# Two transformer blocks with a mixture of experts on one core: expert weights loaded in rows twice as long

## The chip, the core and the metric

The kernel runs on one core of a Trainium2 chip. Its engines work beside each other and wait for each other by semaphores: TensorE (PE in the profile; PEld is its loading of weights), VectorE (DVE), ScalarE (ACT), GpSimd (POOL) and SyncE (SP), which here issues nearly all transfers. Sixteen DMA engines move the data between HBM and SBUF. The metric is the device time of one execution in microseconds (us), the median over runs.

## The reference

Two transformer blocks over 512 tokens of width 1024, in float32. The first has sparse attention and a linear recurrence, the second an mLSTM, differential attention and then a mixture of 32 experts, of which each token takes two. What the change touches is the weights of these experts:

```
def hierarchical_moe(h, w_rg, b_rg, w_re, b_re, w_gate, w_up, w_down):
    hf = h.reshape(-1, d_)
    ...
    for e in range(N_EXPERTS):                       # 32
        act = jax.nn.silu(hf @ w_gate[e]) * (hf @ w_up[e])       # 1024 -> 256, twice
        y = y + combine[:, e:e + 1] * (act @ w_down[e])          # 256 -> 1024
```

The three matrices of one expert are 3.1 MB, those of all 32 are 100.7 MB. Every one is read once.

## The kernel before

The kernel isn't written in the order in which it runs. `Net` records each operation into a `Plan` (`record`, L230), with its price and the tiles that it reads and writes; `Plan.order` (L264) then lays the operations out on five engines by a model of their times, gives each tile a buffer, and `issue` writes the program. There are two such plans here: blocks and the first round of experts in one, and a loop over further rounds that isn't entered with these inputs.

Buffers come from pools by tag (`SIZES`, L525): t4 has 38 buffers of 4 KB per partition, a2 has 15 and p2 has 9 of 2 KB. A tag keeps a list of its free buffers with the time from which each is free, and an operation that gives birth to a tile takes the first. A load may be placed long before its use, as soon as a buffer is free, but leaves twelve free for work that is nearer (`RES`, `NEAR`), from which the expert weights are let off until some 9000 operations ahead (`FREE`, `FAR`, L413). So expert weights are fetched while the second block still runs. A buffer that is taken again holds its load back until the last reader of its former tile is done: SyncE waits for that reader, most often a matmul, and as SyncE issues in order, all loads behind it wait too. Each load also waits until the load eight places before it has landed.

The blocks work on slabs of weights of 0.524 MB: a load on SyncE into a t4 buffer, a rounded copy (hi, F32R) and the remainder (lo, F32R) by ScalarE, VectorE or GpSimd, then three passes on TensorE (`slab`, L588, and `mm3`). Slabs of the second block's input are gt and gr, of its output gr from in_wo; ada_w is summed by VectorE and ScalarE. Mb is a row of the mLSTM's decays, read from DRAM to all partitions (Md).

The experts come last (`experts`, L1796). An iteration does two experts, i and i + 16, each for 64 token rows, beside each other in the halves of TensorE's array:

- GpSimd gathers 128 token rows into X (two buffers in turn), TensorE transposes them, ScalarE and VectorE scale them into XT.
- Up and gate: for each quarter q of the 1024 rows and each expert one load of 128 partitions x 4 KB (wg, 0.524 MB), and four matmuls into H for a quarter. Eight loads per iteration.
- act = silu(gate) x up, two transposes, a copy to aT.
- Down: for each of two k and two halves h of the columns and each expert one load of 128 partitions x 2 KB (wd, 0.262 MB, half of each 4 KB row in DRAM), and two matmuls. Eight loads per iteration, some into p2 and some into a2.
- VectorE scales the result into Y, and GpSimd adds it to the output rows with a scatter (out_rows).

The lines in the profile are nearly all L409, where a recorded call is made; so the names of the tiles tell the operations apart.

Of the kernel before, what the change touches and what calls it, by code (L numbers as in the profile page):

```python
# [134 lines left out]
class Tile:  # L135
    def __init__(self, plan, tag, shape, dt, name, keep, given=None):
        self.plan, self.tag, self.name, self.dt, self.shape, self.keep = plan, tag, name, dt, list(shape), keep
        self.got = given
        self.space = plan.tags[tag].space
        n = 1  # L140
# [29 lines left out]

class Node:
# [7 lines left out]
class Plan:  # L179
# [20 lines left out]
    def tile(self, tag, shape, dt, name, keep=False):  # L200
        return Tile(self, tag, shape, dt, name, keep).view()
# [62 lines left out]
    def order(self):  # L264
# [9 lines left out]
        for nd in nodes:  # L274
            for t in nd.tiles:
                if id(t) in seen or t.tag not in prof:
                    continue
                seen.add(id(t))
                end = N if t.keep else t.last + 1
                start = 0 if t.placed else t.first  # L280
                prof[t.tag][start:end] += 1
# [3 lines left out]
        for nd in nodes:  # L285
            for t in nd.births:
                rest[t.tag] += not nd.load
# [13 lines left out]
        while len(out) < N:  # L301
# [3 lines left out]
            for e, lst in ready.items():  # L305
# [4 lines left out]
                for nd in lst:  # L310
# [7 lines left out]
                    if nd.births:  # L318
                        ok = nd.load or nd.i - p < 400
                        need = {}  # L320
                        for t in nd.births:
# [11 lines left out]
                            s = max(s, tg.free[k - 1][0])  # L333
# [17 lines left out]
            for t in nd.births:  # L351
# [6 lines left out]
                t.slot = tg.free.pop(0)[1]  # L358
                rest[t.tag] -= not nd.load
                if p < t.first:  # L360
                    prof[t.tag][p:t.first] += 1
# [16 lines left out]
            for t in nd.tiles:  # L378
                t.left -= 1
                if t.left == 0 and not t.keep and self.tags[t.tag].space != "dram":  # L380
                    r = max(k.done[1] + (200.0 if k.done[2] == "PE" or t.space == "psum" else 130.0)
                            for k in [nd] + [k for _, k in t.writes + t.reads])
                    insort(self.tags[t.tag].free, (r, t.slot))
                    if p <= t.last:
                        prof[t.tag][p:t.last + 1] -= 1
# [122 lines left out]
class Net:  # L508
    def __init__(self, tc, ctx, I, out, upto="all", dbg=None):
# [5 lines left out]
        self.kept, self.stand = [], {}  # L515
# [9 lines left out]
    SIZES = {"t4": 38, "a2": 15, "p2": 9, "vm": 4, "sq128": 3, "c1k": 4}  # L525

    def start(self):

        self.nc = Plan(self.tc, self.scratch, self.stand)
        self.nc.tag("dram", "dram", [], self.make)  # L530
# [7 lines left out]
    def make(self, t):  # L538
        if t.space == "dram":
            return self.pools["dram"].tile(t.shape, t.dt, name=t.name)  # L540
        return self.pools[t.space].tile(t.shape, t.dt, name=t.name, tag=f"{t.tag}.{t.slot}", bufs=1)

    def tile(self, tag, shape, dt, name, keep=False, bufs=None, space="sbuf"):
        if tag not in self.nc.tags:
            self.bufs.setdefault(tag, bufs or self.SIZES[tag])
            kept = {t.slot for t in self.kept if t.tag == tag}
            self.nc.tag(tag, space, [k for k in range(self.bufs[tag]) if k not in kept], self.make)
        v = self.nc.tile(tag, shape, dt, name, keep)
# [1247 lines left out]
    def experts(self, first=False):  # L1796
# [8 lines left out]
        for i in range(16):  # L1805
# [29 lines left out]
            for k in range(2):  # L1835
                for h in range(2):
                    for e in range(2):
# [169 lines left out]
```

## Time and profile before

| | us |
|---|---|
| median of 3 runs | 1128.71 (1126.05 to 1131.16) |
| profiled execution, own time | 1124.24 |
| its span | 1122.5 |
| TensorE busy | 1042.7 (93%) |
| VectorE busy | 637.7 (57%) |
| ScalarE busy | 393.3 (35%) |
| GpSimd busy | 187.4 (17%) |

The span runs from the first to the last instruction of the program; 1.7 us lie around it. Busy shares are means over stages that are bound by different things, so the slices and the stretches tell more than the table. In the slices each digit is a tenth of a slice of 28 us, 9 for 90% or more. DMA share is the busy time of the 16 DMA engines over the stretch; it can read a little above 1, since records of packets overlap. A matmul of float32 operands has two records, one of F32R operands has one.

### The profile page before, as it was taken

The page shows a single profiled execution, that of the slowest core. Times are in us where ns is not written, and L with a number is a line of the kernel's source. Part 1 is how long each engine was busy: PE and PEld are TensorE (multiplying, and loading weights), DVE is VectorE, ACT ScalarE, POOL GpSimd, SP SyncE. Part 2 cuts the span into 40 slices and gives each one's busy share as a digit, 9 for nine tenths or more (in the row PEclk, how much of TensorE's full clock was granted, in tenths as well). Part 3 has the DMA queues.
Part 4 walks back from the last instruction along what each step waited for, and adds up shares of the span by engine and source line. Part 5 has one row for each costly group of instructions (what it writes and reads, how often), then busy time and mean ns, then how long its engine had stood idle before and what let it go on. Part 6 is the DMA issues. An engine that isn't in the chain of part 4 may idle for free. (4 is left out here: it accounts for less than half of the span.)

```text
span 1122.5 us, 14439 instructions
## 1 busy us (share of the span) xinstructions
PE 1042.7 (93%) x5172; PEld 722.4 (64%) x5172; DVE 637.7 (57%) x1432; ACT 393.3 (35%) x803; POOL 187.4 (17%) x173
## 2 busy tenths in 40 slices
PE   7999999999999999999999999999996999877875
PEld 5776666777887787786677877788785333322221
DVE  4667789786654746977868877444714223222221
ACT  5326566463222326435653433222422112111110
POOL 1201134001110224401211001100301122210101
PEclk9999989999999999999999999999996999999998
DMA  9981100224345717160232433446699899999995
GB/s 339 344 321 49 39 1 20 75 80 150 113 129 180 259 42 279 63 262 11 94 146 85 160 98 107 171 119 233 235 355 356 323 365 351 350 382 345 387 362 181
DMA packets 77375, 223.43 MB, mean 199 GB/s; under 512 B 12165, under 2 KB 13773, under 8 KB 77297
## 3 DMA queue, kind: packets, MB, share of 16 engines
q1 hardware_dynamic: 72688, 214.04, 53.1%
q0 software_dynamic: 4608, 8.40, 3.0%
q8 instruction: 43, 0.70, 0.3%
q14 instruction: 36, 0.29, 0.1%
HBM read 212.91 MB, written 17.32 MB: 205 GB/s over the span
## 5 line engine op out<-in xcount | busy, mean ns | idle before, releaser
L409 PE MATMUL H<-wg,XT 128*64 128x512 f32 x512 | 128.6, 606 | 10.7 <-DMA wg<-in_wgu 7.7
L409 PE MATMUL b<-hTh,gth 128*128 128x512 f32 x464 | 123.0, 402 | 0.0
L409 PE MATMUL b<-hTl,gth 128*128 128x512 f32 x464 | 121.4, 398 | 0.0
L409 PE MATMUL b<-hTh,gtl 128*128 128x512 f32 x464 | 119.4, 396 | 0.0
L409 PEld LDWEIGHTS b<-hTh,gth 128*128 128x128 f32 x464 | 86.4, 189 | 23.7 <-issue 4.2
L409 POOL TENSOR_TENSOR gtl<-gt,gth 128x1024 fp32r<-128x1024 f32 x23 | 57.4, 2498 | 264.5 <-ACT gth L409 243.8
L409 PEld LDWEIGHTS b<-hTh,gtl 128*128 128x128 f32 x464 | 86.6, 188 | 20.5 <-issue 0.5
L409 PEld LDWEIGHTS b<-hTl,gth 128*128 128x128 f32 x464 | 86.2, 188 | 20.0 <-issue 0.9
L409 PEld LDWEIGHTS H<-wg,XT 128*64 128x64 f32 x512 | 38.1, 138 | 86.3 <-issue 51.9
L409 DVE SCALAR_TENSOR_TENSOR ada_acc<-ada_w,cols,ada_acc 128x1024 f32<-128x1024 f32 x42 | 64.7, 1540 | 7.2 <-DMA ada_w<-in_w_ada 7.1
L409 PE MATMUL b<-wd,aT 128*64 128x512 f32 x256 | 61.7, 613 | 7.3 <-ACT aT L409 4.3
L409 DVE TENSOR_SCALAR XT<-b,mod,mod 128x128 f32<-128x128 f32 x64 | 24.2, 407 | 76.7 <-PE H L409 67.2
L409 PE MATMUL b<-grh,hTh 128*128 128x512 f32 x192 | 57.4, 411 | 6.5 <-ACT grh L409 6.5
L409 DVE SCALAR_TENSOR_TENSOR Y<-b,wt,gate 128x512 f32<-128x512 f32 x32 | 23.9, 751 | 69.3 <-PE b L409 63.1
L409 ACT ACTIVATE XT<-b,mod,mod 128x128 f32<-128x128 f32 x64 | 27.3, 456 | 88.8 <-PE H L409 71.6
L409 ACT ACTIVATE gth<-gt 128x1024 fp32r<-128x1024 f32 x53 | 55.3, 1049 | 7.8 <-DMA gt<-in_wb 7.8
L409 PE MATMUL b<-grl,hTh 128*128 128x512 f32 x192 | 56.5, 405 | 0.0
L409 PE MATMUL b<-grh,hTl 128*128 128x512 f32 x192 | 55.5, 402 | 0.0
L409 POOL DMA_INDIRECT out_rows<-Y,si x16 | 25.3, 1583 | 158.6 <-DVE Y L409 145.8
L409 ACT ACTIVATE grh<-gr 128x1024 fp32r<-128x1024 f32 (+1 forms) x39 | 39.9, 1036 | 31.0 <-DVE gr L409 9.4
L409 DVE TENSOR_TENSOR gtl<-gt,gth 128x1024 fp32r<-128x1024 f32 x35 | 42.6, 1223 | 11.1 <-ACT gth L409 10.4
L409 DVE SCALAR_TENSOR_TENSOR mg<-mg,b 128x512 f32<-128x512 f32 x32 | 21.9, 685 | 43.6 <-PE b L409 43.4
(372 smaller groups left out, 1818.3 us busy)
## 6 DMA issues: line engine op xcount, KB each, us to landing
wg<-in_wgu SPq DMA_DIRECT2D x128, 512.0 KB
wd<-in_wd SPq DMA_DIRECT2D x128, 256.0 KB
gt<-in_wb SPq DMA_DIRECT2D x58, 512.0 KB
ada_w<-in_w_ada SPq DMA_DIRECT2D x48, 512.0 KB
gr<-in_wa SPq DMA_DIRECT2D x23, 512.0 KB
wp<-in_wp SPq DMA_DIRECT2D x16, 512.0 KB
gr<-in_wo SPq DMA_DIRECT2D x16, 512.0 KB
cw<-in_cmp_w SPq DMA_DIRECT2D x8, 512.0 KB
```

Source lines behind the costliest of these rows:

```text
L409: i = getattr(getattr(self.nc, eng), meth)(*[val(a) for a in args], **{k: val(v) for k, v in kw.items()})
```

## The change

Up and gate weights are laid out so that one load brings half of the 1024 rows instead of a quarter: 128 partitions x 8 KB, 1.049 MB, four loads per iteration instead of eight. A down load brings whole rows of 4 KB instead of halves: 0.524 MB, four instead of eight. The bytes are the same.

An 8 KB row needs two 4 KB buffers that lie side by side. So the buffers of t4, a2 and p2 become halves of pairs (2k and 2k + 1), for all tiles of these pools and not for the expert weights alone. A tile of width 2 takes a whole pair that is free; a tile of width 1 takes a half, preferably of a pair that is already in use, and a pair holds tiles of one kind at a time, F32R or other. For this a2 goes from 15 to 16 buffers and p2 from 9 to 8. X0 and X1 become one pair, XT and Y another. Everything else is recorded as before, but the plan is made anew with these rules, so that the order of the whole program and the places of its tiles are others.

```diff
+    def fits(self, k, kind):
+        return k >> 1 not in self.live or self.live[k >> 1][0] == kind
...
+    def pick(self, width, taken, kind):
+
+
+        if width == 1:
+            best = None
+            for r, k in self.free:
+                if k not in taken and self.fits(k, kind) and k ^ 1 not in taken:
+                    half = k >> 1 in self.live
+                    if best is None or r == 0.0 and half > best[2]:
+                        best = r, [k], half
+                    if r > 0.0 or half:
+                        break
+            return best and best[:2]
+        seen = set()
+        for r, k in self.free:
+            if k in taken:
+                continue
+            if k ^ 1 in seen:
+                return r, [k & ~1, k | 1]
+            seen.add(k)
+        return None
...
-                            k = need[t.tag] = need.get(t.tag, 0) + 1
+                            k = need[t.tag] = need.get(t.tag, 0) + t.width
+                            got = tg.pick(t.width, {x for g, x in taken if g == t.tag}, t.kind)
...
-                                    or len(tg.free) < k
+                                    or got is None
...
-                            s = max(s, tg.free[k - 1][0])
+                            s = max(s, got[0])
+                            taken.update((t.tag, x) for x in got[1])
...
-    SIZES = {"t4": 38, "a2": 15, "p2": 9, "vm": 4, "sq128": 3, "c1k": 4}
+    UNITS = {"t4": 1024, "a2": 512, "p2": 512}
+    SIZES = {"t4": 38, "a2": 16, "p2": 8, "vm": 4, "sq128": 3, "c1k": 4}
...
+        u = self.UNITS[t.tag]
+        pair, half = divmod(t.slot, 2)
+        if t.gen not in self.pairs:
+            self.pairs[t.gen] = self.pools[t.space].tile([128, 2 * u], F32, name=t.name, tag=f"{t.tag}.{pair}", bufs=1)
+        a = self.pairs[t.gen][:t.shape[0], half * u:half * u + t.row]
...
-            for q in range(4):
+            for q in range(2):
                 ws = []
                 for e in range(2):
-                    ws.append(self.t4("wg", (128, 2, 512)))
+                    ws.append(self.tile("t4", [128, 4, 512], F32, "wg", width=2))
                     nc.sync.dma_start(ws[e], I["wgu"][i + 16 * e, q])
-                for k in range(2):
-                    kt = 2 * q + k
+                for k in range(4):
+                    kt = 4 * q + k
...
             for k in range(2):
-                for h in range(2):
-                    for e in range(2):
-                        w = wd[k, h, e] = self.p2("wd") if k + h + e > 1 and k else self.a2("wd")
-                        nc.sync.dma_start(w, I["wd"][i + 16 * e, k][:, h * 512:(h + 1) * 512])
+                for e in range(2):
+                    w = self.tile("p2" if (4 * i + 2 * k + e) % 3 == 2 else "a2", [128, 2, 512], F32, "wd", width=2)
+                    nc.sync.dma_start(w, I["wd"][i + 16 * e, k])
+                    for h in range(2):
+                        wd[k, h, e] = w[:, h]
...
-        self.X = [self.t4(f"X{k}", keep=True) for k in range(2)]
-        self.XT, self.Y = self.t4("XT", keep=True), self.t4("Y", keep=True)
+        X, Z = [self.tile("t4", [128, 2, 1024], F32, n, True, width=2) for n in ("X", "XTY")]
+        self.X = [X[:, k] for k in range(2)]
+        self.XT, self.Y = Z[:, 0], Z[:, 1]
...
-    d["wgu"] = np.concatenate([wg, wu], axis=2).reshape(32, 4, 2, 128, 512).transpose(0, 1, 3, 2, 4).reshape(32, 4, 128, 1024)
+    d["wgu"] = np.concatenate([wg, wu], axis=2).reshape(32, 2, 4, 128, 512).transpose(0, 1, 3, 2, 4).reshape(32, 2, 128, 2048)
```

Since a pair is one allocation with one name, a tile in its second half bears the name of the tile that came first: in the changed program "gt<-in_w_ada" is a load of ada_w beside a gt, and "gate<-in_wb" one of a gt slab.

On SyncE, at the end of the second block, the first expert weights stand in this order before (in_wo: the block's output slabs; gate5d: a row of gates; xr, x2n: rows of the block's result and of the experts' input, written to DRAM):

```order
L409 DMA gr<-in_wo 128x1024 x7
L409 DMA gate5d<-ada_b 1x256 x4
L409 DMA gate_6994<-gate5d 128x1024
L409 DMA gr<-in_wo 128x1024
L409 DMA wg<-in_wgu 128x1024 x22
L409 DMA wd<-in_wd 128x512
L409 DMA out_rows<-xr_6452 128x1024
L409 DMA x2d<-x2n 128x1024
```

and in this order now:

```order
L458 DMA gr<-in_wo 128x1024 x8
L458 DMA wg<-in_wgu 128x2048
L458 DMA gate5d<-ada_b 1x256 x4
L458 DMA wg<-in_wgu 128x2048
L458 DMA gr<-gate5d 128x1024
L458 DMA wg<-in_wgu 128x2048 x5
L458 DMA out_rows<-gate_3965 128x1024
L458 DMA x2d<-ada_acc 128x1024
L458 DMA wd<-in_wd 128x1024
```

Ahead of the first row copy stood 22 loads of 0.524 MB, and there are seven of 1.049 MB now; the first of them stands a few places earlier.

On SyncE in the middle of the second block, round the first load of Mb, the order was:

```order
L409 DMA gt<-in_wb 128x1024 x2
L409 DMA ada_w<-in_w_ada 128x1024
L409 DMA Mb<-Md 128x512
L409 DMA wd<-in_wd 128x512 x8
L409 DMA gt<-in_wb 128x1024
```

and is now:

```order
L458 DMA gt<-in_wb 128x1024
L458 DMA ada_w<-in_w_ada 128x1024
L458 DMA Mb<-Md 128x512
L458 DMA wd<-in_wd 128x1024 x2
L458 DMA gt<-in_wb 128x1024 x2
L458 DMA wd<-in_wd 128x1024
```

Eight early down loads have become two and then one, with two slabs between them. Mb keeps its place among the loads; the matmul that it waits for is another.

## Rows read from the trace of the kernel before

**Rows 1.** The page: busy tenths, DMA tenths and GB/s in 40 slices.
```profile
PE   7999999999999999999999999999996999877875
...
DMA  9981100224345717160232433446699899999995
GB/s 339 344 321 49 39 1 20 75 80 150 113 129 180 259 42 279 63 262 11 94 146 85 160 98 107 171 119 233 235 355 356 323 365 351 350 382 345 387 362 181
```

**Rows 2.** Stretches: us; PE, PEld, DVE, ACT, POOL busy (count); clock; DMA share; GB/s.
```profile
750.00:800.00 50.00, 50.00 (x223) 39.83 (x222) 29.94 (x32) 14.30 (x18) 7.62 (x4) 1.00 0.58 191
...
820.00:840.00 20.00, 20.00 (x105) 16.80 (x104) 1.64 (x3) 4.03 (x8) 1.57 (x5) 1.00 1.02 409
...
870.00:880.00 10.00, 9.83 (x44) 3.40 (x42) 2.46 (x8) 2.02 (x6) 1.42 (x2) 0.87 0.84 296
...
1010.00:1020.00 10.00, 7.17 (x30) 2.21 (x26) 2.48 (x6) 1.36 (x4) 0.00 (x0) 1.00 0.85 276
...
1050.00:1053.00 3.00, 1.93 (x6) 0.47 (x6) 0.97 (x3) 0.38 (x1) 0.00 (x0) 1.00 1.06 401
...
845.00:1106.00 261.00, 218.59 (x993) 83.28 (x991) 70.27 (x190) 43.63 (x102) 41.44 (x34) 0.95 0.99 361
```

**Rows 3.** DMA queues in 820 to 840 us: packets, MB, share of 16 engines.
```profile
DMA packets 2343, 8.17 MB, mean 409 GB/s; under 512 B 259, under 2 KB 259, under 8 KB 2342
```

**Rows 4.** DMA queues in 1050 to 1053 us.
```profile
DMA packets 657, 1.20 MB, mean 401 GB/s; under 512 B 73, under 2 KB 73, under 8 KB 657
...
q1 hardware_dynamic: 657, 1.20, 105.7%
```

**Rows 5.** DMA queues in 845 to 1106 us; q1 SyncE's, q0 GpSimd's.
```profile
q1 hardware_dynamic: 31321, 85.97, 87.1%
q0 software_dynamic: 4464, 8.01, 12.0%
q8 instruction: 8, 0.13, 0.2%
```

**Rows 6.** SyncE's issues in order of time: start, us, operation, count.
```profile
799.62 31.54 SPq L409 DMA_DIRECT2D wg<-in_wgu  x22
...
815.58 15.58 SPq L409 DMA_DIRECT2D wg<-in_wgu  x15
...
829.68 1.48 SPq L409 DMA_DIRECT2D wg<-in_wgu  x3
...
1005.44 11.63 SPq L409 DMA_DIRECT2D wd<-in_wd  x8
```

**Rows 7.** SyncE's waits in 870 to 884, then 1000 to 1020: us, times, longest.
```profile
SPq L409 <- PE H L409: 15.9, 7, 9.8
...
SPq L409 <- DMA wg<-in_wgu: 9.6, 8, 3.3
```

**Rows 8.** Timeline at the first load of Mb: start, us, engine, operation.
```profile
529.74 0.33 SPq L409 DMA_DIRECT2D Mb<-Md  x1
...
534.55 1.00 ACT L409 ACTIVATE D<-Mb,ifs 128x384 f32<-128x384 f32 x2
```

**Rows 9.** Timeline of the last iteration on TensorE; the page's group of down matmuls.
```profile
1096.07 8.10 PE L409 MATMUL H<-wg,XT 128*64 128x512 f32 x32
...
1106.59 4.10 PE L409 MATMUL b<-wd,aT 128*64 128x512 f32 x16 [0.53 <-ACT aT L409]
...
L409 PE MATMUL b<-wd,aT 128*64 128x512 f32 x256 | 61.7, 613 | 7.3 <-ACT aT L409 4.3
```

**Rows 10.** Timeline: TensorE's first transposes of the expert stage, with its wait.
```profile
867.92 1.94 PE L409 MATMUL b<-ident,X 128*128 128x128 f32 x8 [7.98 <-DMA X<-x2d,si]
```

**Rows 11.** DMA queues in 1010 to 1020 us.
```profile
q0 software_dynamic: 144, 0.30, 15.4%
```

**Rows 12.** The page: SyncE's DMA queue over the whole span.
```profile
q1 hardware_dynamic: 72688, 214.04, 53.1%
```

More of the change, by code (lines that the diff above doesn't have):

```diff
@@ L1 @@
+import itertools
 import math
@@ L135, with __init__ @@
 class Tile:
-    def __init__(self, plan, tag, shape, dt, name, keep, given=None):
+    def __init__(self, plan, tag, shape, dt, name, keep, given=None, width=1):
         self.plan, self.tag, self.name, self.dt, self.shape, self.keep = plan, tag, name, dt, list(shape), keep
-        self.got = given
+        self.got, self.width, self.kind = given, width, dt == F32R
         self.space = plan.tags[tag].space
@@ L168, in __init__, with take, drop @@
         self.free = [(0.0, k) for k in slots]
+        self.live = {}
+    def fits(self, k, kind):
+        return k >> 1 not in self.live or self.live[k >> 1][0] == kind
+    def take(self, slots, kind, count):
+        v = self.live.setdefault(slots[0] >> 1, [kind, 0, None])
+        v[1] += len(slots)
+        if v[2] is None:
+            v[2] = next(count)
+        return v[2]
+    def drop(self, slots):
+        v = self.live[slots[0] >> 1]
+        v[1] -= len(slots)
+        if v[1] == 0:
+            del self.live[slots[0] >> 1]
+    def pick(self, width, taken, kind):
[17 more added lines that the diff above has]
+        return None
 class Node:
@@ L280, in order @@
                 start = 0 if t.placed else t.first
-                prof[t.tag][start:end] += 1
+                prof[t.tag][start:end] += t.width
         for nm, p in prof.items():
@@ L286, in order @@
             for t in nd.births:
-                rest[t.tag] += not nd.load
+                rest[t.tag] += 0 if nd.load else t.width
         ready = {e: [] for e in ("PE", "ACT", "DVE", "POOL", "SP")}
@@ L319, in order @@
                         ok = nd.load or nd.i - p < 400
-                        need = {}
+                        need, taken = {}, set()
                         for t in nd.births:
@@ L357, in order @@
                     continue
-                t.slot = tg.free.pop(0)[1]
-                rest[t.tag] -= not nd.load
+                slots = tg.pick(t.width, (), t.kind)[1]
+                t.gen = tg.take(slots, t.kind, self.count)
+                t.slot = slots[0]
+                tg.free = [x for x in tg.free if x[1] not in slots]
+                rest[t.tag] -= 0 if nd.load else t.width
                 if p < t.first:
-                    prof[t.tag][p:t.first] += 1
+                    prof[t.tag][p:t.first] += t.width
             if e == "ACT" and alt[2] == "activation":
@@ L382, in order @@
                             for k in [nd] + [k for _, k in t.writes + t.reads])
-                    insort(self.tags[t.tag].free, (r, t.slot))
+                    self.tags[t.tag].drop([t.slot + k for k in range(t.width)])
+                    for k in range(t.width):
+                        insort(self.tags[t.tag].free, (r, t.slot + k))
                     if p <= t.last:
-                        prof[t.tag][p:t.last + 1] -= 1
+                        prof[t.tag][p:t.last + 1] -= t.width
             out.append(((s, len(out)), nd, alt))
@@ L514, in __init__ @@
         self.scratch = bacc.Bacc("TRN2", target_bir_lowering=False, num_devices=1)
-        self.kept, self.stand = [], {}
+        self.kept, self.stand, self.pairs, self.count = [], {}, {}, itertools.count()
         self.bufs = {}
```

24 lines of the change are left out of this document (18 added, 6 removed).

## The prediction

> **What bounds the kernel now.** I read the 40 slices first, then a table of stretches, then the DMA packets of three stretches, SyncE's issues and waits, and last the final 20 us. The slices [rows 1] show two kernels in one. Up to about 850 us the PE row stands at 9 and the DMA row between 0 and 8: the two blocks are bound by TensorE, and in the stretch 750 to 800 us it is busy 50.00 of 50.00 us with 223 matmuls, 0.224 us each [rows 2]. From there DMA stands at 9 and PE falls to 7 or 8: the expert stage is bound by its weights, 128 up/gate loads of 0.524 MB and 128 down loads of 0.262 MB, 100.7 MB in all. A change to how these arrive therefore counts from the moment when the transfers become continuous, about 845 us, to the end of the bulk at 1106 us.
>
> In those 261 us the 16 engines are 87.1% busy with SyncE's queue and 12.0% with the gathers and scatters of GpSimd [rows 5], with 0.2% for instructions 99.3%: 259.2 us of engine time. A stretch in which nothing is missing in 820 to 840 reads 1.02 [rows 2], more than 1 because records overlap. So 7 us are lost, in dips of the kind of 870 to 880 (0.84) and 1010 to 1020 (0.85) [rows 2]. Their causes differ. At 870 all buffers are full and SyncE waits 15.9 us in all for up/gate matmuls to free some [rows 7]; around 1010 to 1020 it waits only for landings, 9.6 us for up/gate weights [rows 7], and the eight down loads take 11.63 us to issue [rows 6]: in the built program every load waits until the load eight places before it has landed, and eight down loads are 2.1 MB, about 5 us of work.
>
> **The change part by part.** *Rows of the down weights, 2 to 4 KB.* In 820 to 840 nearly all data packets are 4 KB: 409 GB/s at share 1.02 [rows 2, 3], 401 GB/s at a full share. In 1050 to 1053 they are nearly all 2 KB: 401 GB/s at 1.057 [rows 2, 4], 379. After 845 us the changed kernel has 54 down loads of 0.524 MB left, 28.3 MB: 74.7 us at 379, 70.6 at 401, a gain of 4.1 us.
>
> *Rows of the up/gate weights, 4 to 8 KB.* No row shows an 8 KB packet of this queue. From the two rates, a 4 KB packet takes one engine 4096 / 25.06 = 163.4 ns and a 2 KB packet 86.4, so two halves cost 9.4 ns more than one whole. If an 8 KB row goes as one packet, each spares the same 9.4 ns: 57 loads of 8 rows per engine, 4.3 us. If it is cut in two, nothing. I see no reason that excludes a loss, and bound it by the same 4.3 us. I take the gain, since the packets of 1 to 4 KB all follow the size of their row.
>
> The Trainium skill, "DMA: Bandwidth & Descriptors", section "SWDGE vs HWDGE vs iDMA", speaks against it: it gives a packet as preferably at most 4096 B. By it the 4.3 us fall away. The same page's "Rules for kernel authors" wants at least 1 MiB per DMA for the best bandwidth, which would favour the change far more than I do; with 409 GB/s from loads of half that size [rows 2] the trace leaves little for that rule to give.
>
> *The lag: pairs come free later than single buffers.* This is the term that an eye on the packets alone would miss. Before, 22 up/gate loads stand in SyncE's queue ahead of the first row copies and are issued from 799.62 us on [rows 6], 15 of them within 815.58 to 831.16 [rows 6]. In the changed order only seven stand there, and each needs two neighbours to be free: counted in the built program, their waits end with matmuls 3396, 3401, 3513, 3536, 3537, 3560 and 3560. The load that waits for number 3560 before was issued at 829.68 [rows 6]. So by 845 us, with blocks that run as before, 7 x 1.049 = 7.3 MB of up/gate weights are under way instead of 11.5, and ten down loads of 0.524 MB, 5.2 MB, as before (20 of 0.262). That is 4.2 MB less; one of the row copies, 0.5 MB, stands earlier than it did. Left: 3.7 MB, 9.2 us at 401 GB/s. From 845 us on the queue holds three 1 MB loads at once, and no gap remains.
>
> *What the lag and the size give back.* Being behind, the transfers no longer run into full buffers at 870, and eight loads in flight are 4 to 8 MB. I therefore put the share at 1.02 throughout. Work: 259.2 + 9.2 - 4.1 - 4.3 = 260.0 us, at 1.02 254.9 us instead of 261: 6.1 us less.
>
> *The blocks.* All buffers of the pools t4, a2 and p2 are now halves of pairs, a pair holds either F32 or F32R, and the whole order is made anew. TensorE has the same 4247 matmuls, and their order is nearly kept. But loads stand closer to their use: of SyncE's loads in the blocks, 41 have fewer than 70 matmuls between the one they wait for and the one that needs them, where 19 had. At 0.224 us 70 matmuls are 15.7 us. All but two still have 30 or more, 7 us, for a chain of landing, split on ScalarE and use. The one that looks late is the first load of Mb: 12 matmuls instead of 25. It was issued at 529.74 and first read at 534.55 [rows 8]; issued after matmul 2307 instead of 2294 it comes some 4 us later, and ScalarE waits in order in front of work that TensorE needs. I take 2 us for all of these; ends 0 and 8, the upper one from four loads that are late by 2 us each.
>
> *The end.* The last up/gate bytes release twice as many matmuls: the four pairs of the second half of the rows, not two. A set of eight pairs takes 8.10 us [rows 9], so two more cost 2.0 us. The down matmuls, 4.10 us with a short wait for weights among them [rows 9], against 3.86 on average (61.7 us over 16 iterations [rows 9]), then find theirs landed: 0.5 us less at most. Net 1.5 us. The start of the stage, where TensorE stands 7.98 us for the first gather [rows 10], may shift by the last row copy, queued behind larger loads; transfers go on meanwhile, so it costs nothing.
>
> *Sum.* -6.1 + 2 + 1.5 = -2.6 us. The profiled execution took 1124.24 us (span 1122.5), so 1121.6; the median of the runs shown is 4.5 us above the profiled execution, and from it the forecast is 1126.1, say 1126.
>
> **The rivals.** About 0.5% (5.6 us) is what a measurement of this kernel can tell from no change.
>
> *The gaps stay.* If the dips are the gathers' doing (q0 has 12.0% of the engines' time [rows 5]) and not the short queue's, the share stays 0.993: 260.0 / 0.993 = 261.8 us, +0.8, with blocks and end +4.3: 1133. For it: in 1010 to 1020 their queue has 15.4% [rows 11]. Against: the stage holds 32 of them and far fewer dips.
>
> *The change doesn't do what it says.* If rows of 8 KB travel as 4 KB packets, work is 264.3 us, at 1.02 259.1: -1.9 + 3.5 = +1.6, 1130. This is what the Trainium skill's packet size above would make of it.
>
> *Slower: weights late in the blocks.* The place is the second block, 500 to 800 us, where TensorE never rests in the stretch shown [rows 2] and every late slab moves the end one for one, since row copies, routing and the lagging prefetch all hang on TensorE's position. For it: 41 short distances instead of 19; ScalarE and VectorE split slabs in order. It decides from about 9 us of stops: at 12 us the sum is -6.1 + 12 + 1.5 = +7.4, 1136. Against: 30 matmuls are 7 us, and before the loads landed and were split in less.
>
> *Faster by more.* If the share reaches 1.04, as in short stretches (1.06 in 1050 to 1053 [rows 2]), and the blocks lose nothing: 260.0 / 1.04 = 250, -11 + 1.5 = -9.5, 1119.
>
> **How the numbers follow.** Forecast (1122 to 1130) 0.40; gaps stay 0.14; rows cut 0.13; late slabs 0.15; faster by more 0.18. Faster by over 0.5%, below 1123.1: all of the last and a quarter of the forecast's, 0.28. Slower, above 1134.4: late slabs and a part of the gaps that stay, 0.20. Within: 0.52. The range leaves out a tenth at either side: 1115 to 1138, the lower end from a share of 1.04 with 4 us more from early buffers, the upper from late slabs.
>
> **What would show it.** Right: packets of 8 KB on SyncE's queue, and fewer of them, some 54,000 instead of 72,688 [rows 12]; a share near 1.02 between 850 and 1100 without dips; fewer bytes moved by 845 us; SyncE waiting there for matmuls, later for landings only; TensorE idle a little more between 370 and 390, 530 and 545 us. Wrong: an idle stretch in the DMA row after 860 us (pairs that come free too late in the expert stage itself), TensorE waiting for weights in the blocks, or up/gate loads issued ahead of 799 us in number, which would turn the lag into a lead.

## The result, and the profile after

The changed kernel takes 1190.14 us, median of 6 runs (1186.90 to 1193.91), the kernel before 1127.03 in runs of the same chips: a ratio of 1.056, 95% interval 1.0536 to 1.0585. The forecast was 1126, its range ended at 1138. The profiled execution of after took 1188.14 us, 63.9 more than that of before, its span 63.6 more. Four moments of the two traces tell where these lie. Number 3690 is the first of the last twenty small matmuls of the routing, counted along TensorE's 4247; behind them TensorE waits for the first gather.

| us from the start of the span | before | after | stretch before | stretch after | difference |
|---|---|---|---|---|---|
| number 3690, the blocks' end | 855.5 | 900.7 | 855.5 | 900.7 | +45.2 |
| first transposes of the experts | 867.9 | 918.5 | 12.4 | 17.8 | +5.4 |
| last packet of weights | 1109.2 | 1147.9 | 241.3 | 229.4 | -11.9 |
| end of the span | 1122.5 | 1186.1 | 13.3 | 38.2 | +24.9 |

So the transfers of the expert stage, for which the change was made, do take less time. The loss lies before and behind them. The page of after, the rows that answer to [rows 1]:

```profile
PE   7999899999999899799899999998894999785990
...
PEclk9998998999999999899899999999896999897995
DMA  9862100113434726251241523345569999999952
```

Slices are 30 us here. The PE row has eights and sevens between slices 5 and 30, where before it stood at 9; the last slice is a 0, in which DMA still has a 2. Stretches, with the columns of [rows 2]: the whole way to number 3690 in before and in after, then four of after.

```profile
0.00:855.50 855.50, 827.50 (x4225) 644.58 (x4225) 574.34 (x1292) 354.57 (x709) 145.50 (x141) 0.99 0.45 155
```

```profile
0.00:900.70 900.70, 843.63 (x4225) 654.64 (x4225) 578.38 (x1307) 354.67 (x706) 132.87 (x129) 0.97 0.41 142
...
820.00:840.00 20.00, 13.46 (x56) 9.73 (x55) 13.58 (x17) 5.41 (x7) 7.52 (x4) 0.83 0.98 368
...
900.00:920.00 20.00, 6.03 (x28) 5.91 (x28) 2.23 (x12) 0.37 (x2) 2.29 (x2) 0.50 1.01 417
920.00:940.00 20.00, 19.94 (x91) 6.88 (x91) 4.99 (x12) 3.40 (x10) 3.61 (x3) 0.94 0.92 352
940.00:1100.00 160.00, 131.47 (x593) 46.63 (x591) 35.58 (x83) 25.02 (x63) 26.67 (x21) 0.91 1.02 397
```

The first two lines hold the same 4225 matmul records. TensorE is idle for 57.1 us instead of 28.0, which is 29.1 of the 45.2. The other 16.1 are busy time. The granted clock, a share of 2.4 GHz, is 0.97 on average instead of 0.99, and 2% of 843.63 us are 17. Behind longer stops it stands at the lower of its two levels (1.2 GHz): at 0.50 in 900 to 920, where TensorE waits for the first gather, and 0.83 in 820 to 840 is a mean of both. Not every stop did this; behind one of 2.10 us at 275.86 it stayed at 1.00. At the lower level the same matmuls take longer. In 940 to 1100 the DMA engines read 1.02 at 397 GB/s, where the whole stage before had 0.99 and 361 [rows 2].

**Where the blocks stop.** SyncE's issues in after, 799 to 830 us (start, us, operation, count):

```profile
799.61 6.42 SPq L458 DMA_DIRECT2D gt<-in_wb  x2
806.09 0.43 SPq L458 DMA_DIRECT2D gt<-in_w_ada  x1
812.98 0.33 SPq L458 DMA_DIRECT2D wp<-in_wp  x1
818.97 0.33 SPq L458 DMA_DIRECT2D ada_w<-in_w_ada  x1
...
821.91 7.61 SPq L458 DMA_DIRECT2D gr<-in_wo  x8
```

VectorE in the same time, with its idle time and what ended it:

```profile
804.45 1.23 DVE L458 TENSOR_TENSOR grh<-gt,gtl 128x1024 fp32r<-128x1024 f32 x1 [4.32 <-ACT gtl L458]
...
811.63 1.28 DVE L458 SCALAR_TENSOR_TENSOR ada_acc<-gt,cols,ada_acc 128x1024 f32<-128x1024 f32 x1
...
817.72 1.23 DVE L458 TENSOR_TENSOR grl<-wp,gtl 128x1024 fp32r<-128x1024 f32 x1 [4.81 <-ACT gtl L458]
```

Read the ends against the issues. 804.45 + 1.23 = 805.68, and the second gt<-in_wb goes out at 805.71; 811.63 + 1.28 = 812.91, wp at 812.98; 817.72 + 1.23 = 818.95, ada_w at 818.97. Each time SyncE stood until VectorE had read an earlier slab. In the built program these five loads share one pair, and the load at 799.61 and the three that these times name each wait for a reader of the other half, the neighbour, whose bytes they don't overwrite. Their own halves had been free 2.2, 5.8, 1.2 and 5.7 us before, or the load ahead had only then gone out: 14.9 us of waiting for a neighbour, 12.7 of them in the 19.4 us from 799.61 to 818.97. TensorE still runs without a gap up to 825; it stops when it comes to the work that hangs on the last of these loads and on the eight of in_wo, which stand behind them in SyncE's order:

```profile
820.00:825.00 5.00, 5.00 (x24) 4.02 (x23) 0.74 (x1) 0.00 (x0) 1.85 (x2) 1.00 0.84 225
```

```profile
824.26 1.28 DVE L458 SCALAR_TENSOR_TENSOR ada_acc<-ada_w,cols,ada_acc 128x1024 f32<-128x1024 f32 x1 [4.71 <-DMA ada_w<-in_w_ada]
...
829.50 0.38 PE L458 MATMUL b<-rt,ones 128*128 128x36 f32 x2 [3.12 <-ACT mg L458]
...
830.55 1.22 DVE L458 TENSOR_TENSOR gr<-gr,gate 128x1024 f32<-128x1024 f32 x1 [0.83 <-DMA gr<-in_wo]
...
832.92 2.08 PE L458 MATMUL b<-mh,ybl 128*128 128x512 f32 x4 [3.03 <-ACT mh L458]
...
843.35 0.74 PE L458 MATMUL b<-ybl,mh 128*128 128x512 f32 x2 [2.28 <-ACT ybl L458]
```

VectorE stood 4.71 us for ada_w, the load of 818.97, and the first stop of TensorE (3.12 us) hangs on what VectorE and ScalarE do behind that. The second (3.03) hangs on the first slab of in_wo, the third (2.28) on ScalarE's copy of a later one. In before the loads of in_wo began 45 us earlier, and TensorE ran on without a stop (20.00 of 20.00 us in 820 to 840 [rows 2]):

```profile
777.12 13.07 SPq L409 DMA_DIRECT2D gr<-in_wo  x7
```

A pair is one tile for the framework that sets the waits, under the name of the tile that came first. While it lives its halves are told apart. When both are done and a half is taken again, a new tile begins, and its first write waits for the last reader of the whole old tile. The planner counts the halves as free one by one. By the built programs, 78 of the 357 loads of after wait, directly or through another engine, for a later matmul than their own bytes ask for (foreign waits below), 3441 matmuls in sum; before it was 4 loads and 72 matmuls. Set against the trace (the end of the operation waited for, less the later of the last reader of the load's own bytes and the issue of the load ahead), SyncE was held in this way for 365.6 us of the 900, by 55 loads with over 0.5 us each; in before for 22.5 us, by 4. Most of this cost TensorE nothing, as in 800 to 825: its idle time grew by 29.1 us. The longest stop of the blocks, 7.49 us at 494.69, has the same look: a late slab of in_wa keeps ScalarE, which works in order, 4.52 us from a result on which VectorE's next chain hangs. The smaller stops were not traced one by one.

```profile
481.97 1.07 ACT L458 ACTIVATE grl<-gr 128x1024 fp32r<-128x1024 f32 x1 [4.52 <-DMA gr<-in_wa]
...
494.69 1.11 PE L458 MATMUL b<-ident,dq 128*128 128x128 f32 x4 [7.49 <-DVE dq L458]
```

**Where the end goes.** VectorE behind the last weights in after:

```profile
1149.34 0.88 DVE L458 SCALAR_TENSOR_TENSOR act<-act,H 128x256 f32<-128x256 f32 x2 [10.97 <-ACT act L458]
1150.14 1.40 DVE L458 SCALAR_TENSOR_TENSOR XTY<-b,wt,gr 128x512 f32<-128x512 f32 x2
1158.16 1.41 DVE L458 SCALAR_TENSOR_TENSOR XTY<-b,wt,gr 128x512 f32<-128x512 f32 x2 [6.62 <-DMA out_rows<-XTY,si]
1166.40 1.41 DVE L458 SCALAR_TENSOR_TENSOR XTY<-b,wt,gr 128x512 f32<-128x512 f32 x2 [6.83 <-DMA out_rows<-XTY,si]
1174.04 1.41 DVE L458 SCALAR_TENSOR_TENSOR XTY<-b,wt,gr 128x512 f32<-128x512 f32 x2 [6.23 <-DMA out_rows<-XTY,si]
```

Four iterations' Y stand behind the last gate (act) in VectorE's order. There is one Y, so each waits until the scatter of the one before has read it: four rounds of 8 us. Behind the last gate of before stood one:

```profile
1104.63 0.88 DVE L409 SCALAR_TENSOR_TENSOR act<-act,H 128x256 f32<-128x256 f32 x2 [7.56 <-ACT act L409]
1109.46 0.75 DVE L409 SCALAR_TENSOR_TENSOR Y<-b,wt,gate 128x512 f32<-128x512 f32 x1 [3.96 <-PE b L409]
```

**The first gather.** GpSimd waits for the last row copy, which SyncE issued at 896.61:

```profile
909.81 1.30 POOL L458 DMA_INDIRECT X<-x2d,si  x1 [14.41 <-DMA x2d<-x2n]
```

That is 13.2 us from copy to gather; before it was 9.2 (851.50 to 860.65). TensorE's wait answers to [rows 10]:

```profile
918.45 1.94 PE L458 MATMUL b<-ident,X 128*128 128x128 f32 x8 [13.31 <-DMA X<-x2d,si]
```

**The packets.** The page of after, the row that answers to [rows 12]:

```profile
q1 hardware_dynamic: 54256, 214.03, 48.7%
```

Packets of 8192 B stand among them: an 8 KB row is one packet. Worked out from all packet records behind the first transposes: 8 KB took 321.2 ns on average (6390 packets, median 309), 4 KB 163.8 (6656); in before 4 KB took 167.4 (12,398, median 159) and 2 KB 89.0 (13,312).

### The profile page after: what moved, and what is told of

The parts are those of the page before. It is cut to its first block, busy times and chain, and to the rows that moved or that the text cites. A ratio compares the mean times of both kernels' runs of the same rounds, so it can differ in the third digit from the quotient of the medians.

```text
span 1186.1 us, 14193 instructions
## 1 busy us (share of the span) xinstructions
PE 1054.7 (89%) x5172; PEld 734.2 (62%) x5172; DVE 639.0 (54%) x1448; ACT 391.7 (33%) x799; POOL 174.8 (15%) x161
## 3 DMA queue, kind: packets, MB, share of 16 engines
q1 hardware_dynamic: 54256, 214.03, 48.7%
## 5 line engine op out<-in xcount | busy, mean ns | idle before, releaser
L458 PE MATMUL H<-wg,XTY 128*64 128x512 f32 x512 | 126.0, 628 | 10.1 <-DVE XTY L458 9.2
L458 PEld LDWEIGHTS H<-wg,XTY 128*64 128x64 f32 x512 | 37.9, 143 | 79.8 <-issue 64.4
L458 PE MATMUL b<-hTh,gth 128*128 128x512 f32 x282 | 79.0, 403 | 0.0
L458 PEld LDWEIGHTS b<-hTh,gth 128*128 128x128 f32 x282 | 52.8, 189 | 13.3 <-issue 1.8
L458 PE MATMUL b<-hTh,gtl 128*128 128x512 f32 x220 | 59.7, 396 | 0.0
L458 PEld LDWEIGHTS b<-hTh,gtl 128*128 128x128 f32 x220 | 41.3, 188 | 10.3 <-issue 0.7
L458 PEld LDWEIGHTS b<-grh,hTh 128*128 128x128 f32 x216 | 40.3, 189 | 11.2 <-ACT grh L458 1.9
L458 DVE SCALAR_TENSOR_TENSOR ada_w<-ada_w,cols 128x1024 f32<-128x1024 f32 x20 | 27.1, 1357 | 20.4 <-DMA ada_w<-in_w_ada 20.4
L458 ACT ACTIVATE P<-P,nst 128x512 f32<-128x512 f32 (+3 forms) x60 | 33.1, 555 | 9.8 <-DVE nst L458 8.5
L458 PEld LDWEIGHTS b<-ident,X 128*128 128x128 f32 x128 | 14.4, 146 | 31.6 <-issue 25.7
L458 POOL TENSOR_TENSOR gtl<-gt,gth 128x1024 fp32r<-128x1024 f32 x8 | 20.8, 2602 | 66.1 <-ACT gth L458 60.3
```

What stands on the lines that cost most here:

```text
L458: i = getattr(getattr(self.nc, eng), meth)(*[val(a) for a in args], **{k: val(v) for k, v in kw.items()})
```

## The experiments

Two theories stood first. Theory 1: pools whose pairs can't mix kinds leave fewer buffers, so the slabs come late. Theory 2: the 1 MB loads hold the slabs up. Chance was the third: any new order costs something. Theory 4, the tile that two halves share, came after the first four runs, which are pairs_singles, pairs_halves, after_scatter and before_16_8. The table has the moments of every profiled execution; medians and ratios are against runs of the kernel before on the same chip.

| kernel | median us | ratio, 95% | number 3690 | first transposes | last weights | span |
|---|---|---|---|---|---|---|
| after | 1190.14 | 1.056 (1.0536 to 1.0585) | 900.7 | 918.5 | 1147.9 | 1186.1 |
| pairs_singles | 1187.24 | 1.0542 (1.0510 to 1.0575) | 907.7 | 920.3 | 1168.2 | 1184.5 |
| pairs_halves | 1184.46 | 1.0513 (1.0486 to 1.0539) | 900.0 | 914.2 | 1166.8 | 1181.7 |
| after_scatter | 1177.43 | 1.0434 (1.0399 to 1.0469) | 901.7 | 919.7 | 1159.2 | 1176.1 |
| before_16_8 | 1131.21 | 1.0050 (1.0025 to 1.0074) | 859.5 | 872.0 | 1115.2 | 1128.3 |
| rule_only | 1138.57 | 1.0116 (1.0069 to 1.0163) | 864.9 | 878.1 | 1122.2 | 1134.9 |
| wd_only | 1132.71 | 1.0060 (1.0036 to 1.0084) | 868.4 | 881.4 | 1117.3 | 1131.0 |
| keep_aware | 1142.84 | 1.0149 (1.0104 to 1.0195) | 854.5 | 873.1 | 1101.8 | 1140.0 |
| keep_aware_sc | 1128.66 | 1.0020 (0.9995 to 1.0045) | 856.8 | 877.0 | 1113.7 | 1128.4 |
| ka_halves | 1133.47 | 1.0069 (1.0047 to 1.0091) | 857.9 | 871.9 | 1117.8 | 1131.6 |
| short_q6 | 1128.72 | 1.0022 (0.9999 to 1.0044) | 851.1 | 864.8 | 1106.8 | 1122.7 |
| before_scatter | 1129.21 | 1.0022 (1.0002 to 1.0042) | 854.3 | 866.8 | 1111.1 | 1124.4 |
| wd_keep_sc | 1125.54 | 1.0004 (0.9988 to 1.0020) | 860.1 | 872.9 | 1108.5 | 1123.0 |

**pairs_singles**: the changed pools with the old loads.

```diff
-                    ws.append(self.tile("t4", [128, 4, 512], F32, "wg", width=2))
+                    ws.append(self.t4("wg", (128, 2, 512)))
...
-                    w = self.tile("p2" if (4 * i + 2 * k + e) % 3 == 2 else "a2", [128, 2, 512], F32, "wd", width=2)
...
+                        w = wd[k, h, e] = self.p2("wd") if k + h + e > 1 and k else self.a2("wd")
```

> The changed pools (pairs of one kind, X and XTY as pairs), but the expert weights fetched as before: 128 loads of 0.524 MB and 128 of 0.262 MB in single buffers. Theory 1, the pools: TensorE reaches the routing (the small matmuls ahead of the first gather, number 3690) at about 900 us as in the changed kernel, not at 855.5, since the slabs of the blocks come as late as there; VectorE's order writes Y in turn with the gates, so the end is as before: 1127 + 45 less some 5 us that the transfers make up, about 1165 us. Theory 2, the size of the loads: the 1 MB weights are what holds the slabs up; number 3690 back at about 856 us and 1128 us in all.

The size of the loads is not the cause: with the old loads number 3690 comes at 907.7, later still. The end is as before (16.3 us behind the last weights). But the time isn't the 1165 us that theory 1 gave: the blocks lost 7 us more than in after, the size of one stop of TensorE just ahead of number 3690 (7.28 us, up to 906.53), and the stage took 247.9 us from the first transposes to the last weights, 6.6 more than in before with the same loads.

**pairs_halves**: the changed kernel, each load cut in two.

```diff
-                    nc.sync.dma_start(ws[e], I["wgu"][i + 16 * e, q])
+                    for h in range(2):
+                        nc.sync.dma_start(ws[e][:, 2 * h:2 * h + 2], I["wgu"][i + 16 * e, q][:, 1024 * h:1024 * h + 1024])
...
-                    nc.sync.dma_start(w, I["wd"][i + 16 * e, k])
                     for h in range(2):
+                        nc.sync.dma_start(w[:, h], I["wd"][i + 16 * e, k][:, h * 512:(h + 1) * 512])
```

> The changed kernel with each load cut in two: rows of 4 and 2 KB again, each half of a pair by a load of its own. Theory 1, the pools: number 3690 at about 900 us; Y is written in turn with the gates in VectorE's order, so the last 25 us of the changed kernel go; the transfers lose the gain of the large rows, some 5 to 9 us: about 1170 us. Theory 2, the size of the loads: blocks as before, 1128 us.

The blocks stay late without any large load. 1184 instead of 1170 us: the end got its 23 us back (14.9 instead of 38.2), the transfers lost as much (252.6 us instead of 229.4). By estimate 7 of these 23 us are 2.9 MB more that were still to come and some 11 the large rows; the rest may be the scatters that had stood behind the last weights.

**after_scatter**: the planner's count of a gather or scatter.

```diff
-                bus = max(bus, s + dur + (650.0 if e == "SP" else 4800.0)) + byts / 360.0
-                end = bus + 910.0
+                if e == "SP":
+                    bus = max(bus, s + dur + 650.0) + byts / 360.0
+                    end = bus + 910.0
+                else:
+                    bus += byts / 360.0
+                    end = s + dur + 4800.0 + byts / 360.0 + 910.0
```

> The changed kernel, but the planner counts a gather or scatter from its own issue, and no longer behind all weights that it has queued. Rows and pools are those of the change. In VectorE's order the last four iterations' Y then stand in turn with the gates; in the changed kernel eight Y operations stand behind the last gate. Theory 1, the end: 38 us from the last weights to the end become 13, so 25 us less: about 1165 us; the blocks stay late (number 3690 near 900 us). Rival: the four scatters wait for something else than their place in the order, or TensorE falls behind for want of weights: 1185 to 1190 us, the end as long as before.

The end is normal again, 16.9 us: the place in the order was its cause. The median gained 12.7 us, not 25, since the last weights came 11.3 us later. Part of that had only been put off: three scatters that had stood behind the weights now share the engines with them. The share from the first transposes to the last weights also fell, from 0.97 to 0.95.

**before_16_8**: `"a2": 16, "p2": 8` in the kernel before.

> The kernel before with 16 buffers a2 and 8 p2 instead of 15 and 9, nothing else: no pairs, single loads. Rival 3, chance: that any new layout of the order costs some tens of us in the blocks; then number 3690 is reached 10 us or more later and the time is 1140 us or above. Theory 1: only the rule of pairs does that; number 3690 within 4 us of 855.5 and 1127 us, within 6.

This new order costs 4 us, not 45, as theory 1 had it. One new order doesn't exclude chance; rule_only and keep_aware, new orders too, do so for the main part of the loss.

**rule_only**: pairs_singles, but each buffer a tile of its own.

```diff
-        if t.tag not in self.UNITS:
+        if True:
             return self.pools[t.space].tile(t.shape, t.dt, name=t.name, tag=f"{t.tag}.{t.slot}", bufs=1)
...
-        X, Z = [self.tile("t4", [128, 2, 1024], F32, n, True, width=2) for n in ("X", "XTY")]
-        self.X = [X[:, k] for k in range(2)]
-        self.XT, self.Y = Z[:, 0], Z[:, 1]
+        self.X = [self.t4(f"X{k}", keep=True) for k in range(2)]
+        self.XT, self.Y = self.t4("XT", keep=True), self.t4("Y", keep=True)
```

> As pairs_singles (single loads of 4 and 2 KB rows, 38, 16 and 8 buffers, the planner gives the halves of a pair to one kind alone), but each buffer is a tile of its own again, as before. Theory 4, the shared tile: a pair is one tile for the framework that sets the waits, so the first write into a new pair waits for the last reader of both old halves; counted in the built programs, 120 loads of pairs_singles and 78 of the changed kernel wait for a matmul that doesn't use their bytes, 4 in the kernel before and 4 here. By it number 3690 is reached at 856 to 862 us and the time is 1127 to 1135 us. Theory 1, the rule that kinds don't mix: as pairs_singles, number 3690 at 900 us or later and 1180 us or above.

This settles it between theories 1 and 4. The rule and the loads are those of pairs_singles, and 48.7 us of its loss are gone; only the shared tiles, X and XTY among them, were taken out. SyncE is held by foreign readers for 19.1 us, in pairs_singles for 350.7, and TensorE is idle in the blocks for 29.7 us, in after for 57.1:

```profile
0.00:864.90 864.90, 835.18 (x4225) 650.79 (x4225) 574.44 (x1307) 353.03 (x705) 135.62 (x130) 0.98 0.44 151
```

The rule costs some too: number 3690 is 9.4 us late, 5.4 more than in before_16_8, and the time lies 3.6 us above the range that was expected.

**wd_only**: the down weights alone, t4 as before.

> Only the down weights in 4 KB rows and pairs (a2 and p2 in pairs, 16 and 8); up/gate weights and the 38 buffers t4 as before. 6 of its loads wait for a matmul that doesn't use their bytes. Theory 4: the blocks are those of before_16_8 (number 3690 at 859.5 us), and the transfers gain the 6 us that 4 KB rows spare (416 rows per engine, 163.8 ns instead of 2 x 89): about 1125 us. Theory 1: the rule of kinds costs in these two pools too: number 3690 at 870 us or later and 1137 us or above.

Neither theory's figures: number 3690 at 868.4, 9 us later than in before_16_8, and 1133 us. The rule and six loads with foreign waits in two small pools seem to cost more than the rows gave; this run doesn't tell the two apart.

**keep_aware**: large rows and pairs as in the change, with two edits to the pairs: a pair stays the same tile while its kind stays, and a pair that changes its kind counts as free when both halves are. The choice among free buffers was written anew for this; these are the lines that matter most.

```diff
+        if v[1] == 0 and v[0] != kind:
+            v[0], v[2] = kind, None
...
     def drop(self, slots):
         v = self.live[slots[0] >> 1]
         v[1] -= len(slots)
-        if v[1] == 0:
-            del self.live[slots[0] >> 1]
...
+            if width == 2 or v and not v[1] and v[0] != kind:
+                r = max(r, at[k ^ 1])
```

> The changed kernel with its large rows and pairs, but a pair stays the same tile as long as its kind stays, and the planner counts a pair that changes its kind as free only when both halves are; 9 loads instead of 78 still wait for a matmul that doesn't use their bytes, 48 matmuls in all instead of 3441. The last Y operations still stand behind the last gates. Theory 4: number 3690 at 856 to 864 us, transfers as fast as in the changed kernel, its long end: 1140 to 1150 us. Theory 1: number 3690 near 900 us, 1185 us.

Theory 4 again: the time is within its range, and number 3690 at 854.5 comes 1.5 us ahead of it and earlier than in before, with the rule of kinds, the pairs (X and XTY too) and the 1 MB loads all in place. SyncE is held for 51.3 us, and TensorE is idle in the blocks for 25.7:

```profile
0.00:854.50 854.50, 828.82 (x4225) 645.11 (x4225) 579.50 (x1301) 351.04 (x703) 158.02 (x138) 0.99 0.44 152
```

SyncE in the stretch that answers to 799 to 822 of after: the eight loads of in_wo (three in the line shown, the others by 787) begin at 771.47, 20 us ahead of matmul 3400 (791.8), where after had them 4 us ahead of it (821.91, 826.0).

```profile
753.39 1.46 SPq L452 DMA_DIRECT2D gt<-in_wb  x2
760.96 0.33 SPq L452 DMA_DIRECT2D gt<-in_w_ada  x1
765.14 0.33 SPq L452 DMA_DIRECT2D gt<-in_wp  x1
766.34 0.33 SPq L452 DMA_DIRECT2D gt<-in_w_ada  x1
...
771.47 13.02 SPq L452 DMA_DIRECT2D gt<-in_wo  x3
```

**keep_aware_sc**: keep_aware with the edit of after_scatter.

> keep_aware, and as in after_scatter the planner counts a gather or scatter from its own issue. Theory 4: blocks as before and the gain of the large rows kept, about 11 us of engine time, with a normal end: 1117 to 1128 us. after_scatter gained 13 us of the 25 that its end had cost, as the bulk of the transfers ended 11 us later: if that holds here too, 1130 to 1135. Theory 1: 1172 us or above.

Another 14.2 us, at the end (38.2 us became 14.7). Both losses are undone, and the time is that of the kernel before within its interval (0.9995 to 1.0045). It lies between the two ranges expected: the last weights came 11.9 us later, as in after_scatter. So the gain of the large rows is still lost somewhere.

**ka_halves**: keep_aware_sc with each load cut in two, as in pairs_halves.

> keep_aware_sc with each load cut in two again (rows of 4 and 2 KB, half the bytes per load), on the same pairs; 12 loads wait for a matmul that doesn't use their bytes, as good as its 9. The row's price alone: by the packets of before and after (8 KB in 321 ns against 2 x 167, 4 KB in 164 against 2 x 89) the large rows spare some 13 us over 128 + 128 loads, 11 of them after the first gather. Theory: the transfers after the first gather take 11 us more engine time than in keep_aware_sc; of it less reaches the end, since smaller loads leave fewer gaps: 1132 to 1140 us. Rival: rows don't matter to the end, since the stage isn't bound by their time but by the gaps: 1129, as keep_aware_sc.

The time is within the theory's range. Pools and pairs are the same, so the rows' price can be seen nearly alone. All packets from 800 us on take 303.4 us per engine (99.5 MB of SyncE's), in keep_aware_sc 287.1 (99.6 MB): 16.3 us spared, of which 4.8 arrive in the median (ratios 1.0069 and 1.0020). That is more than the 13 worked out; a 4 KB packet took 171.8 ns on average here and 167.4 in before. Stretches of ka_halves, then of keep_aware_sc:

```profile
860.00:880.00 20.00, 10.21 (x44) 5.90 (x45) 2.44 (x10) 1.50 (x4) 3.27 (x3) 0.59 0.97 377
880.00:900.00 20.00, 19.83 (x100) 7.35 (x96) 6.12 (x15) 5.07 (x13) 3.67 (x3) 1.00 0.99 354
```

```profile
860.00:880.00 20.00, 4.22 (x18) 3.37 (x20) 2.04 (x10) 1.51 (x4) 3.07 (x3) 0.50 0.81 323
880.00:900.00 20.00, 19.83 (x95) 7.05 (x92) 4.15 (x11) 2.70 (x8) 2.83 (x3) 0.98 0.80 305
```

The large loads lose 20 x (0.16 + 0.19) = 7 us of the engines' time in these 40 us: the buffers are full, and SyncE stands 25.0 us for up/gate matmuls in 850 to 905 of keep_aware_sc (11.2 in ka_halves). In keep_aware_sc TensorE starts 5.1 us later.

```profile
SPq L456 <- PE H L456: 25.0, 4, 19.4
```

**short_q6**: keep_aware_sc, fewer weights ahead of the row copies.

```diff
                     s = max(f, nd.est)
+                    if e == "SP" and nd.load and nd.tiles[0].name in FREE:
+                        s = max(s, bus - 6000.0)
```

> keep_aware_sc, but the planner places a load of expert weights no earlier than 6 us before the modelled end of what is queued ahead of it. Between the first and the last of the four row copies to x2d stand 2 up/gate loads in SyncE's queue instead of 6. In keep_aware_sc the first gather was issued 18.8 us after the last row copy (853.98 to 872.80), in the kernel before 9.2 us (851.50 to 860.65). Theory: the row copy waits for the megabytes queued ahead of it; with four loads fewer, 4.2 MB or 10 us at 401 GB/s, the first gather follows 9 to 12 us after the last row copy, TensorE starts 7 to 10 us earlier, and 3 to 8 us of it reach the end: 1121 to 1126 us. Rival: the gather waits for something else, and the weights that now come later cost what is gained: 1128 to 1135 us.

The gather comes 9.2 us after the last row copy (847.07 to 856.23) and waits for VectorE's slots now, not for the copy:

```profile
872.80 1.29 POOL L456 DMA_INDIRECT X<-x2d,si  x1 [21.23 <-issue]
```

```profile
856.23 1.29 POOL L458 DMA_INDIRECT X<-x2d,si  x1 [10.37 <-DVE wt L458]
```

The first line is keep_aware_sc, where the profile names no event that ended the wait; the second is short_q6. In ka_halves, with six loads between the copies but half the bytes in each, it was 11.1 us (853.73 to 864.84). So the delay goes with the bytes ahead of the row copy, as the theory had it. TensorE starts 12.2 us earlier (864.8), 5.7 of them since the blocks ended earlier, but none of it reaches the median, which lies in the rival's range. At the first transposes 79.6 MB were still to come instead of 77.6, 5 us at 401 GB/s, and the stage took 242.0 us instead of 236.7. The dip of keep_aware_sc is there too, although TensorE had started earlier:

```profile
860.00:880.00 20.00, 13.83 (x58) 5.70 (x60) 3.41 (x10) 3.79 (x10) 1.97 (x2) 0.72 0.80 324
880.00:900.00 20.00, 20.00 (x100) 7.32 (x98) 5.55 (x11) 3.72 (x9) 4.27 (x3) 1.00 0.82 300
```

So the late gather isn't the dip's cause; it goes with the 1 MB loads, and ka_halves lacks it. The profiled execution of short_q6 was 5.8 us faster than that of keep_aware_sc while the medians are the same, so the rest of the account stays open.

**before_scatter**: the kernel before with the edit of after_scatter.

> The kernel before, with the planner's new count of gathers and scatters and nothing else. Its Y already stand in turn with the gates. Theory: no change beyond 4 us, 1122 to 1130 us: the price mattered only with the larger queue of the change. Rival: the new count alone is worth 5 us or more, and what keep_aware_sc gained on keep_aware isn't the end's: 1120 us or below.

No change beyond 4 us, as expected: the count matters only with the larger queue of the change.

**wd_keep_sc**: wd_only with the edits of keep_aware and after_scatter.

> Only the down weights in 4 KB rows and pairs, as in wd_only, with the two changes to the planner of keep_aware_sc (a pair stays the same tile while its kind stays; gathers and scatters counted from their own issue); up/gate weights as before. 4 loads wait for a matmul that doesn't use their bytes, as before. Theory: blocks as before (number 3690 at 854 to 859 us, 868 in wd_only), and the 4 KB rows spare 416 x (2 x 89 - 164) ns = 5.8 us per engine in the transfers, with no coarser buffers for the up/gate weights and so no new gap at the start of the stage: 1119 to 1124 us, faster than the kernel before. Rival: what the rows spare goes into gaps, as in keep_aware_sc (16 us of engine time spared, nothing of it in the time): 1126 to 1131 us.

The transfers took 235.6 us from the first transposes to the last weights instead of 241.3: 5.7 us less, the 5.8 that were worked out. The blocks ended 4.6 us later, 1.1 beyond their range, and the time is that of before within 0.2%: it misses the theory's range and comes close to the rival's. No kernel here beats the one before.

## Why the prediction was wrong, step by step

**What bounds the kernel** held: the blocks by TensorE, the stage by the weights. That is why the 45.2 us that the blocks lose, stops and longer matmuls, move the end nearly one for one.

**Rows of the down weights**: forecast 4.1 us. 2 x 89.0 - 163.8 = 14.2 ns per row, 416 rows per engine from the first transposes on, 5.9 us. The mechanism was right, the size a third too small.

**Rows of the up/gate weights**: forecast 4.3 us. 2 x 167.4 - 321.2 = 13.6 ns, 399 rows, 5.4 us. The 54,000 packets forecast were 54,256. So the rival that rows are cut falls. The Trainium skill, "DMA: Bandwidth & Descriptors", section "SWDGE vs HWDGE vs iDMA", gives a packet as preferably at most 4096 B, in its table on what GpSimd prepares. On SyncE's queue this trace has packets of 8192 B, and one costs less than two of 4096 B.

**The lag**: forecast 9.2 us, by bytes under way at 845 us. At the first transposes after had 79.6 MB of weights still to come, before 78.1: 1.5 MB, 3.7 us at 401 GB/s. The blocks were late by more than the loads, so the loads caught up.

**The share of 1.02**: right from 940 to 1100. Two dips were left: 0.92 in 920 to 940, and the last 11 us before the end of the weights, 0.27, which lose 8 us of the engines' time with TensorE busy for 10.43 of 10.90 us. The DMA row of 918 to 1148 us shows it in the last two of its 40 slices, of 5.75 us each:

```profile
DMA  9799999999999999999999999999999999999950
```

**The blocks** were the step that failed: 2 us, with 8 as the upper bound, against 45.2. The late slabs were named as the rival with a chance of 0.15, and TensorE waiting for weights in the blocks as a sign of being wrong; that is what came. Whether the late loads are those on the list of 41 short distances was not traced load by load. Two things were wrong. The cost was worked out load by load, "30 matmuls are 7 us" for landing and split, as if each load had this time to itself; the loads hang on each other, and SyncE, which issues in order, stood 365.6 us for neighbours. And the reason that so many loads stood close to their use was not looked for. It is for the most part in the pairs themselves and not in the planner's rules, with which rule_only was 9.4 us late; a comparison of what each load waits for with who uses its bytes would have shown the 78 foreign waits ahead of any run. The stops also cost clock, 16.1 us of longer matmuls, of which the prediction had nothing.

**The end**: 1.5 us against 24.9. TensorE's last matmuls were costed, VectorE's order wasn't read: eight Y operations behind the last gate. The mechanism is the planner's: it lets a scatter land only behind all weights queued, and twice the bytes per load in the same ring of eight puts it further off; so Y goes later in the order. after_scatter and keep_aware_sc bear that out.

**The first gather**: "it costs nothing", against +5.4 us to the first transposes. The Trainium skill, the same page, section "Queues, rings and completion order", has the descriptors of one queue consumed in ring order on each engine. This trace agrees: the copy at 853.98 in keep_aware_sc, with some 6 MB of weights ahead, was followed by its gather 18.8 us later, the one of ka_halves, with half of that, 11.1 us, the one of short_q6 9.2 us later. Transfers did go on during the wait (1.01 in 900 to 920 of after); but TensorE started 5.4 us later than the end of the blocks explains, and the share is 0.92 in the 20 us behind.

**The sum** with what was measured: 45.2 + 5.4 - 11.9 + 24.9 = 63.6 us. The stage's part, -11.9, was forecast as -6.1, counted from 845 us.

## What to carry to other kernels

Before buffers are joined into larger tiles, compare for each load what it waits for with who last used its bytes. A wait on the neighbour's reader turns a pool into a chain, and the loads that stand behind it in order pay. When loads grow and their number in flight stays, all that queues behind them (row copies, gathers, and the planner's idea of them) moves too: read the order of every engine at the end, not the bound one's alone. A gain in the transfers is worth only what the buffers let through: 16.3 us of engine time were spared here and 4.8 arrived.

## What the runs showed of the hardware

8 KB rows travel whole on SyncE's queue: 321.2 ns on average against 2 x 167.4 for 4 KB, medians 309 and 159, and 84 for 2 KB. So doubling a row spares about 9 ns per row in the medians from 2 to 4 KB as from 4 to 8 KB. A row copy of 0.5 MB with six up/gate loads of 1 MB issued in the 8 us ahead of it was followed by its reader 18.8 us later; with six of 0.5 MB 11.1 us later; with two of 1 MB between the first copy and it 9.2 us later, and then the reader waited for something else. A stop of TensorE costs beyond itself: with 29.1 us more idle time in the blocks and a granted clock of 0.97 instead of 0.99, the same matmuls took 16.1 us longer.
